# One layer of a hybrid mLSTM/HGRN2 block on one core: later use of the mixers' outputs, three blocks of merge gates computed first, small work moved to ScalarE

## The chip, the cores and the metric

The kernel runs on one core of a Trainium2 chip. A core has TensorE (PE, matrix products into PSUM), VectorE (DVE), ScalarE (ACT) and GpSimd (POOL), which run apart from each other and meet through semaphores, and a queue (SP) that issues transfers from memory. The metric is the device time of one execution in microseconds. Before the change it is 2555.0 us, the median of three runs (2554.29 to 2555.2).

## What is computed

The reference is one decoder layer in fp32 on 256 positions of width 2048:

```
x = x + 0.5 * swiglu(rmsnorm(x), ffn1)                       # inner width 5632
h = rmsnorm(x)
mq,mk,mv,mo,mi,mf,hq,hf,hi,hg,gate_m,gate_h = split(h @ w_in) # 2048 x 11272
y_m = mlstm_mixer(mq,mk,mv,mo,mi,mf)       # causal conv on q,k; 4 heads; 1024 wide
y_h = hgrn2_mixer(hq,hf,hi,hg)             # f = lb+(1-lb)*sigmoid(hf); 8 heads; 1024 wide
merged = sigmoid(gate_m)*(y_m @ w_proj_m) + sigmoid(gate_h)*(y_h @ w_proj_h)
x = x + merged @ w_out
x = x + cross_attention(rmsnorm(x), rmsnorm(mem))            # 4 heads of 512, 256 memory rows
x = x + 0.5 * swiglu(rmsnorm(x), ffn2)
out = rmsnorm(x)
```

Both mixers are written as scans over chunks. mLSTM weights a score q·k by an exponential of running sums of log forget gates, and divides by a guarded row sum. HGRN2 does the same with one decay for each of its 128 channels.

## The kernel before, in words

**Products.** Every large product has the 256 positions as rows (two blocks of 128, so two PSUM tiles `pa`) and 512 columns of the weight at a time. Each fp32 operand is split into a high and a low part, and three products stand for one: high·high, high·low, low·high (lines 248, 249, 250). Weights come by SP in tiles `wr` of four k-tiles (1 MB); each half of such a tile, two k-tiles, is one **group**: ACT casts it to the high part `wh`, DVE subtracts to get the low part `wl`, and PE then runs 2 k-tiles x 2 row blocks x 3 products = 12 matmuls on it. `wh` and `wl` have four buffers each, and a group is split three ahead of its use. There are 904 groups, counted here from 0: 264 for the first FFN, 264 to 511 for the mixer, 512 to 639 for cross attention, 640 to 903 for the second FFN. In the mixer: f and q of HGRN2 264 to 295, its v and g to 327, the mLSTM output gate in three narrower blocks of 344 columns 328 to 351, mLSTM q, k, v 352 to 383, then four merge blocks of 24 groups each from 384 (8 for `gm`, 8 for `gh`, 4 for y_h @ w_proj_h, 4 for y_m @ w_proj_m), and w_out from 480.

**The other operand** is needed transposed, as a pair `oh`, `ol`. `turn_on_vector` makes it from a 128x512x2 tile with 16 DVE transposes of 32x256 into `tt` (four pieces of four), then an ACT pass for `oh` and a DVE pass for `ol`. `written` holds the recording back until a pair that a matmul asks for has its instructions recorded.

**Order of the work around the products.** The kernel is recorded by a planner in Python. After each group `tick` adds the group's estimated PE time and lets small pieces in: pieces with a due time (`timed`), and a queue (`bg`) of mixer pieces, up to three for each group. Both only go in while the estimated backlog of DVE and ACT is under 2 us. The estimate is kept by `Paced`: a base and a time per element for each instruction of DVE and of ACT. What a piece records on PE, DVE and ACT then lies between the weight splits. A scheduler then assigns buffers and may still shift single instructions. All engines run in their recorded order.

**The pieces that matter here.** `hgrn_levels` (the decays, products `qc` with `kt`), `hgrn_out` (`hsq`, `hss`, `rstd` on POOL, then `g`, and the turn of y_h in two pairs), `mlstm_weights` (for each head: `di` = identity x input gate, `r0` and `r1` from it, four matmuls, then `ew`; `di`, `r0`, `r1` have one buffer each), `conv` (`mq`, `mk`), `mlstm_scores`, `mlstm_out` (the heads' `mo`, and the turn of y_m in two pairs). Right after the gates of merge block 0 a step calls `flush`: all pieces that are left are recorded there at once. Long-lived tiles (norm operands, y pairs, gates, `tt`) share one pool `s4` of 22 buffers.

Of the kernel before, what the change touches and what calls it, by code (L numbers as in the profile page):

```python
# [14 lines left out]
AF = mybir.ActivationFunctionType  # L15
ALU = mybir.AluOpType
# [3 lines left out]
P = 128  # L20
# [79 lines left out]
class Core:  # L100
    def __init__(self, nc):
        self.tensor, self.gpsimd, self.sync = nc.tensor, nc.gpsimd, nc.sync
        self.vector, self.scalar = Paced(nc.vector, 0.13, 0.00106), Paced(nc.scalar, 0.22, 0.00082)


class Block:
# [71 lines left out]
    def next_timed(self):  # L178
        i = min(range(len(self.timed)), key=lambda i: self.timed[i][0])
        self.timed.pop(i)[1]()  # L180

    def flush(self):
        while self.timed or self.bg:
            if self.timed:
                self.next_timed()
            else:
                self.bg.popleft()()

    def load(self, u, parts=1):
        if u.raw is None:  # L190
# [32 lines left out]
        self.flush()  # L223

    def gemm_nat(self, ops, wap, n0, n, evac, kts=None, row0=0, late=0):

        nc = self.nc
        box = {}  # L230
        pairs = ops
        nkt = 4 * len(pairs) if kts is None else kts

        def mm_for(k0, nk):
            def mm(hi, lo, ts=(0, 1)):
                if k0 == 0:
                    box["ps"] = [self.pacc([P, n]) for _ in range(2)]
                if k0 >= nkt - 2 * late and len(ts) == 2:
                    ts = (0,)
                    box.setdefault("late", []).append(lambda: mm(hi, lo, (1,)))  # L240
                for j in range(nk):
                    kt = k0 + j
                    xh, xl = self.written(pairs[kt // 4])
                    for t in ts:
                        sl = slice(t * P, (t + 1) * P)
                        a_h, a_l = xh[:, kt % 4, sl], xl[:, kt % 4, sl]
                        o = box["ps"][t]
                        nc.tensor.matmul(o, a_h, hi[:, j, :], start=(kt == 0), stop=False)  # L248
                        nc.tensor.matmul(o, a_h, lo[:, j, :], start=False, stop=False)  # L249
                        nc.tensor.matmul(o, a_l, hi[:, j, :], start=False, stop=(kt == nkt - 1))  # L250
            return mm

        for k0 in range(0, nkt, 4):
            u = Unit(wap, row0 + k0 * P, 4, n0, n, 2)
            for q in range(2):
                self.steps.append(Sub(u, q, mm_for(k0 + 2 * q, 2)))
        if not late:
            self.do(lambda: evac(box["ps"]))
            return

        def finish():
            evac(box["ps"], (0,))
            for f in box["late"]:
                f()
            evac(box["ps"], (1,))
        self.do(finish)
# [27 lines left out]
        self.unwritten[id(p)] = p  # L294
        return p

    def written(self, p):

        while id(p) in self.unwritten:
            self.next_timed()  # L300
        return p

    def turn_later(self, src, gain, dst, ticks=1):
        self.after(ticks, lambda: self.turn(src, gain, dst, (0,)))
# [137 lines left out]
    def rstd_of(self, ss, n, dim):  # L442
        nc = self.nc
        ms = self.sm(n, "ms")
        nc.vector.tensor_scalar(ms, ss, 1.0 / dim, EPS, op0=ALU.mult, op1=ALU.add)
        r = self.sm(n, "rstd", tag=f"rstd{n}")
        nc.gpsimd.tensor_tensor(r, ms, self.mhalf[:, :n], op=ALU.pow)  # L447
        return r

    def squares(self, src, ss_col):  # L450
# [79 lines left out]
    def mixer(self, norm, chunk_done):  # L530
        nc, a = self.nc, self.a
        w = a["w_in"][0]
        ops = LazyOps(lambda: norm().ops)
# [77 lines left out]
        self.do(lambda: self.bg.extend(self.mlstm_out(M, MV, MO)))  # L611


        merged = [None] * 4
        G = {}
        for c in range(4):
            for key, base in (("gm", 7176), ("gh", 9224)):
                def evac_g(ps, key=key):
                    r = norm().rstd
                    G[key] = self.t4([P, 2, 512], name=key)  # L620
                    for t in range(2):
                        nc.scalar.activation(G[key][:, t, :], ps[t], AF.Sigmoid, scale=r[:, t:t + 1])
                self.gemm_nat(ops, w, base + 512 * c, 512, evac_g)
            if c == 0:
                self.do(lambda: self.flush())

            def evac_h(ps):
                for t in range(2):
                    nc.vector.tensor_mul(G["gh"][:, t, :], ps[t], G["gh"][:, t, :])

            def evac_m(ps, c=c):
                gm, gh = G["gm"], G["gh"]
                for t in range(2):
                    nc.vector.tensor_mul(gm[:, t, :], ps[t], gm[:, t, :])
                    nc.vector.tensor_add(gm[:, t, :], gm[:, t, :], gh[:, t, :])
                merged[c] = self.pair()
                if c < 3:
                    self.turn_on_vector(gm, None, merged[c])
                else:
                    self.turn_later(lambda t: gm[:, t, :], None, merged[c])  # L640

            self.gemm_nat(LazyOps(lambda: self.Y["h"], 2), a["w_proj_h"][0], 512 * c, 512, evac_h)
            self.gemm_nat(LazyOps(lambda: self.Y["m"], 2), a["w_proj_m"][0], 512 * c, 512, evac_m)
        for c in range(4):
            def evac(ps, c=c):
                self.add_to_x(c, ps, 1.0, lambda: chunk_done(c))
            self.gemm_nat(LazyOps(lambda: merged, 4), a["w_out"][0], 512 * c, 512, evac)

    def hgrn_levels(self, h, b):


        nc = self.nc
# [9 lines left out]
        def prep_f():  # L662
            f = h["f"]
            for i in range(4):
                hd = 4 * b + i
                nc.vector.tensor_scalar(f[:, i, :], f[:, i, :], self.oml[:, hd:hd + 1], self.lb[:, hd:hd + 1],
                                        op0=ALU.mult, op1=ALU.add)

        def prep_k():
            S["k"] = self.t4([P, 4, T], name="k")  # L670
# [128 lines left out]
    def mlstm_weights(self, m):  # L799

        nc = self.nc
# [15 lines left out]
        def head(h):  # L817
            lf = [m["lf"][:, t, h:h + 1] for t in range(2)]
            ig = [gs[:, t, h:h + 1] for t in range(2)]
            di = self.small.tile([P, P], F32, name=self.nm("di"), tag="di", bufs=1)  # L820
            r0 = self.small.tile([P, 129], F32, name=self.nm("r0"), tag="r0", bufs=1)
            r1 = self.small.tile([P, 257], F32, name=self.nm("r1"), tag="r1", bufs=1)
            for t, r, o in ((0, r0, 0), (1, r1, 129)):
                nc.vector.tensor_scalar(di, self.ident, ig[t], None, op0=ALU.mult)
                nc.vector.scalar_tensor_tensor(r[:, o:o + P], in0=self.gt, scalar=lf[t], in1=di,
                                               op0=ALU.mult, op1=ALU.add)
            nc.vector.tensor_copy(r0[:, 128:129], lf[0])
            nc.vector.tensor_copy(r1[:, 0:129], lf[1].broadcast_to([P, 129]))
            p0 = self.ps([P, 129])
            p1 = self.ps([P, 257])  # L830
            nc.tensor.matmul(p0, self.le, r0, start=True, stop=True)
# [12 lines left out]
        return [logs] + [lambda h=h: head(h) for h in range(4)]  # L844

    def mlstm_scores(self, m):
# [330 lines left out]
```

## Time and profile before

| | before |
|---|---|
| median of 3 runs | 2555.0 us |
| profiled execution, its own time | 2555.04 us |
| its span, first to last instruction | 2553.2 us |
| PE busy | 2528.8 us, 99% |
| DVE busy | 1730.7 us, 68% |
| ACT busy | 1201.8 us, 47% |
| DMA, mean share of 16 engines | 57% |
| mean granted TensorE clock | 0.998 |

A busy PE is not PE at its peak: a matmul's shown duration (0.39 us) is longer than the distance to the next (0.227 us), so a stretch can be full and still slow. The number of matmuls in a stretch tells more than its busy time. A window's row has, after the stretch, its length, and for each engine the busy time with the number of instructions in brackets, then the granted clock, the DMA share and GB/s.

In this profile group 364 starts at 1016.8 us, group 405 at 1145.2 us, and the scores of the first attention head at 1575.4 us.

### The profile page before, as it was taken

What the parts mean: (1) busy time and instruction counts of PE and PEld (TensorE: products, weight loads), DVE (VectorE), ACT (ScalarE), POOL (GpSimd) and SP (SyncE); (2) the same over time, 40 slices, a digit from 0 to 9 for tenths busy, and PEclk for the clock granted to TensorE, in tenths of its full rate; (3) what the DMA queues carried; (4) which work ended last, traced back from release to release, by engine and by line L of the source; (5) the groups of instructions that cost most, each with busy time, mean ns of one, the idle gap of its engine ahead of it and who ended that gap; (6) DMA issues with size and microseconds to landing.
All of it is one profiled execution on the core that took longest, in us unless ns stands there. A gap on an engine that the chain in (4) does not pass through costs nothing.

```text
span 2553.2 us, 29044 instructions
## 1 busy us (share of the span) xinstructions
PE 2528.8 (99%) x11431; PEld 2104.7 (82%) x11431; DVE 1730.7 (68%) x2384; ACT 1201.8 (47%) x1385; POOL 13.5 (1%) x21
## 2 busy tenths in 40 slices
PE   8999999999999999999999999999999999999998
PEld 7888888888888898787888888888888888888887
DVE  5767644767768878967666787677767574457664
ACT  5444434444455565644444454444544443344443
POOL 0000000000000000000000000000000000000000
PEclk9999999999999999999999999999999999999999
DMA  7665565565555545545555565555566556555653
GB/s 262 197 193 189 195 198 190 189 198 190 193 190 185 176 138 165 183 163 181 190 191 197 187 212 180 170 175 173 190 198 190 191 196 197 188 192 194 214 189 128
DMA packets 243305, 479.92 MB, mean 188 GB/s; under 512 B 8008, under 2 KB 14432, under 8 KB 243168
## 3 DMA queue, kind: packets, MB, share of 16 engines
q1 hardware_dynamic: 242016, 476.15, 57.4%
q10 hardware_dynamic: 1152, 1.92, 0.2%
q8 instruction: 89, 1.46, 0.2%
q14 instruction: 48, 0.39, 0.0%
HBM read 475.94 MB, written 2.10 MB: 187 GB/s over the span
## 4 chain that ended last, share of the span: by engine, by line
PE 92%; DVE 6%; issue 1%; ACT 0%; DMA 0%; POOL 0%; SPq 0%; POOLq 0%; ACTq 0%
PE pa L250 30%; PE pa L248 30%; PE pa L249 30%; DVE wl L90 2%; DVE tt L90 2%; PE ps L726 1%; DVE ol L90 1%; DVE cv L90 0%; PE ps L277 0%; DMA x<-in_x 0%; PE ps L966 0%; PE ps L967 0%; PE ps L965 0%; POOL rstd L447 0%; ACT kn L90 0%
## 5 line engine op out<-in xcount | busy, mean ns | idle before, releaser
L90 DVE TENSOR_TENSOR wl<-wr,wh 128x1024 fp32r<-128x1024 f32 (+1 forms) x904 | 1094.2, 1213 | 721.6 <-ACT wh L90 715.0
L90 ACT CAST wh<-wr 128x1024 fp32r<-128x1024 f32 (+1 forms) x904 | 942.0, 1045 | 1141.9 <-PE pa L250 1091.3
L248 PE MATMUL pa<-wh,oh 128*128 128x512 f32 (+1 forms) x3616 | 1409.7, 390 | 7.0 <-ACT oh L90 4.4
L249 PE MATMUL pa<-wl,oh 128*128 128x512 f32 (+1 forms) x3616 | 1403.6, 388 | 2.3 <-DVE wl L90 2.3
L250 PE MATMUL pa<-wh,ol 128*128 128x512 f32 (+1 forms) x3616 | 1402.5, 388 | 0.2 <-DVE ol L90 0.2
L248 PEld LDWEIGHTS pa<-wh,oh 128*128 128x128 f32 x3616 | 680.0, 188 | 143.3 <-ACT oh L90 4.8
L249 PEld LDWEIGHTS pa<-wl,oh 128*128 128x128 f32 x3616 | 680.2, 188 | 141.1 <-DVE wl L90 5.5
L250 PEld LDWEIGHTS pa<-wh,ol 128*128 128x128 f32 x3616 | 679.7, 188 | 138.8 <-DVE ol L90 0.7
L90 DVE STREAM_TRANSPOSE tt<-sil 32x256 f32<-32x256 f32 x352 | 153.6, 436 | 6.8
L90 DVE STREAM_TRANSPOSE tt<-x 32x256 f32<-32x256 f32 x144 | 62.8, 436 | 2.8
L90 ACT CAST oh<-tt 128x1024 fp32r<-128x1024 f32 x29 | 30.6, 1054 | 39.7 <-DVE tt L90 39.7
L90 ACT ACT_TABLE_LOAD x34 | 43.6, 1283 | 10.1 <-DVE rs L90 3.1
L90 ACT ACTIVATE oh<-tt,cols 128x256 fp32r<-128x256 f32 x52 | 23.3, 500 | 47.7 <-DVE tt L90 47.7
L90 ACT ACTIVATE sil<-pa,rstd 128x512 f32<-128x512 f32 x44 | 29.8, 689 | 17.8 <-PE pa L250 17.7
L90 DVE TENSOR_TENSOR ol<-tt,oh 128x1024 fp32r<-128x1024 f32 x29 | 35.4, 1220 | 1.6 <-ACT oh L90 1.4
L90 DVE STREAM_TRANSPOSE tt<-kn 32x256 f32<-32x256 f32 x64 | 27.9, 436 | 5.6 <-ACT kn L90 4.5
L90 DVE SCALAR_TENSOR_TENSOR sil<-pa,rstd,sil 128x512 f32<-128x512 f32 x44 | 31.0, 743 | 0.0
L90 DVE STREAM_TRANSPOSE qt<-qn 32x256 f32<-32x256 f32 x64 | 27.9, 436 | 4.1 <-ACT qn L90 3.0
L90 ACT ACTIVATE oh<-ps,cols 128x256 fp32r<-128x256 f32 x44 | 20.3, 473 | 21.4 <-DVE ol L90 15.6
L90 DVE COPY_PREDICATED at<-cst,ps 128x128 f32<-128x128 int32 x80 | 22.8, 328 | 10.6 <-PE ps L726 10.0
L90 ACT ACTIVATE junk<-x 128x512 f32<-128x512 f32 x40 | 24.9, 625 | 7.6 <-DVE x L90 7.0
L90 DVE SCALAR_TENSOR_TENSOR ol<-ps,cols,oh 128x256 fp32r<-128x256 f32 x44 | 20.7, 480 | 10.8 <-ACT oh L90 10.5
(174 smaller groups left out, 649.4 us busy)
## 6 DMA issues: line engine op xcount, KB each, us to landing
wr<-in_ffn_w SPq DMA_DIRECT2D x263, 1024.0 KB, 5.2
wr<-in_w_in SPq DMA_DIRECT2D x80, 1024.0 KB, 5.1
wr<-in_xattn_wkv SPq DMA_DIRECT2D x32, 1024.0 KB, 5.4
wr<-in_w_out SPq DMA_DIRECT2D x16, 1024.0 KB, 5.1
wr<-in_xattn_wq SPq DMA_DIRECT2D x16, 1024.0 KB, 5.0
wr<-in_xattn_wo SPq DMA_DIRECT2D x16, 1024.0 KB, 5.1
wr<-in_w_in SPq DMA_DIRECT2D x12, 688.0 KB, 4.1
wr<-in_w_proj_h SPq DMA_DIRECT2D x8, 1024.0 KB, 5.0
```

The lines of the kernel that those rows point to most:

```text
L90: return fn(out, *args, **kw)
L248: nc.tensor.matmul(o, a_h, hi[:, j, :], start=(kt == 0), stop=False)
L249: nc.tensor.matmul(o, a_h, lo[:, j, :], start=False, stop=False)
L250: nc.tensor.matmul(o, a_l, hi[:, j, :], start=False, stop=(kt == nkt - 1))
L726: nc.tensor.matmul(ps[:, i, :], kt[:, g, j * P:(j + 1) * P], S["qc"][:, 2 * g + j, :], start=True, stop=True)
```

## The change

1. `flush` after the first merge gates is gone. `written` now takes the list and an index; while the pair isn't there, or not recorded yet, it records one more waiting piece (`next_piece`) and looks again.
2. The merge is split in `gates(c)` and `merge(c)`. The order becomes gates 0, 1, 2, merge 0, gates 3, merge 1, 2, 3. `gm` and `gh` are kept for each block, so up to six gate tiles live at once instead of two. y_h @ w_proj_h now starts at group 432 instead of 400.
3. `Paced` has new constants (DVE 0.19 + 0.00104 n instead of 0.13 + 0.00106 n; ACT 0.25 + 0.00085 n instead of 0.22 + 0.00082 n), and `rstd_of` adds 0.9 to DVE's estimate for the trip to POOL. Nothing that runs is changed by this directly, but the planner puts the pieces elsewhere.
4. 24 instructions go from DVE to ACT: `f` = lb + (1-lb)f (8 of 128x256), `di` (8 of 128x128), and the copies of `lf` into `r0` (4 of 128x1) and `r1` (4 of 128x129). ACT gets one ACT_TABLE_LOAD more, 35 instead of 34.

PE's number of instructions is the same.

```diff
-        self.vector, self.scalar = Paced(nc.vector, 0.13, 0.00106), Paced(nc.scalar, 0.22, 0.00082)
+        self.vector, self.scalar = Paced(nc.vector, 0.19, 0.00104), Paced(nc.scalar, 0.25, 0.00085)
...
+    def next_piece(self):
+        if self.timed:
+            self.next_timed()
+        else:
+            self.bg.popleft()()
...
-                    xh, xl = self.written(pairs[kt // 4])
+                    xh, xl = self.written(pairs, kt // 4)
...
-    def written(self, p):
-
-        while id(p) in self.unwritten:
-            self.next_timed()
-        return p
+    def written(self, ops, i):
+
+        while ops[i] is None or id(ops[i]) in self.unwritten:
+            self.next_piece()
+        return ops[i]
...
         nc.gpsimd.tensor_tensor(r, ms, self.mhalf[:, :n], op=ALU.pow)
+        nc.vector.end += 0.9
...
-        for c in range(4):
+        def gates(c):
             for key, base in (("gm", 7176), ("gh", 9224)):
                 def evac_g(ps, key=key):
                     r = norm().rstd
-                    G[key] = self.t4([P, 2, 512], name=key)
+                    g = G[key, c] = self.t4([P, 2, 512], name=key)
...
-            if c == 0:
-                self.do(lambda: self.flush())
...
+        for c in range(3):
+            gates(c)
+        merge(0)
+        gates(3)
+        for c in range(1, 4):
+            merge(c)
...
-                nc.vector.tensor_scalar(f[:, i, :], f[:, i, :], self.oml[:, hd:hd + 1], self.lb[:, hd:hd + 1],
-                                        op0=ALU.mult, op1=ALU.add)
+                nc.scalar.activation(f[:, i, :], f[:, i, :], AF.Identity, scale=self.oml[:, hd:hd + 1],
+                                     bias=self.lb[:, hd:hd + 1])
...
-                nc.vector.tensor_scalar(di, self.ident, ig[t], None, op0=ALU.mult)
+                nc.scalar.activation(di, self.ident, AF.Copy, scale=ig[t])
...
-            nc.vector.tensor_copy(r0[:, 128:129], lf[0])
-            nc.vector.tensor_copy(r1[:, 0:129], lf[1].broadcast_to([P, 129]))
+            nc.scalar.copy(r0[:, 128:129], lf[0])
+            nc.scalar.copy(r1[:, 0:129], lf[1].broadcast_to([P, 129]))
```

How the recorded order moves is shown at three places, on DVE. A `wl` row is the weight split of one group, so the rows between two `wl` are what the planner put in between. Digits behind a name are buffer numbers.

**The first place** is the end of HGRN2, from the split of group 361 in the kernel before: `hss`, `ms`, `g` are the head norm of one row block, `tt<-g` the transposes of y_h.

```order
L90 TENSOR_TENSOR wl_7383<-wr_7259,wh_7382 128x1024
L90 TENSOR_REDUCE hss_7372<-hsq_7370 128x4
L90 TENSOR_SCALAR ms_7374<-hss_7372 128x4
L90 SCALAR_TENSOR_TENSOR g_6673<-ps_7365,rstd_7376,g_6673 128x128 x4
L90 TENSOR_TENSOR wl_7422<-wr_7301,wh_7421 128x1024
L90 TENSOR_REDUCE hss_7409<-hsq_7407 128x4
L90 TENSOR_SCALAR ms_7411<-hss_7409 128x4
L90 SCALAR_TENSOR_TENSOR g_6673<-ps_7398,rstd_7413,g_6673 128x128 x4
L90 STREAM_TRANSPOSE tt_7487<-g_6673 32x2x4x32
```

Now, from the split of group 368:

```order
L90 TENSOR_TENSOR wl_7461<-wr_7377,wh_7460 128x1024
L90 TENSOR_TENSOR wl_7498<-wr_7377,wh_7497 128x1024
L90 TENSOR_REDUCE hss_7487<-hsq_7485 128x4
L90 TENSOR_SCALAR ms_7489<-hss_7487 128x4
L90 SCALAR_TENSOR_TENSOR g_6443<-ps_7476,rstd_7491,g_6443 128x128 x4
L90 TENSOR_TENSOR wl_7516<-wr_7419,wh_7515 128x1024
L90 STREAM_TRANSPOSE tt_7554<-g_6443 32x2x4x32 x4
L90 STREAM_TRANSPOSE cv_7559<-k_7533 32x2x4x32 x3
```

Before, both head norms of y_h's second pair stood in neighbouring groups (361 and 362), ahead of 32 transposes, 16 of that pair and 16 of the conv input (`cv<-q`). Now the piece there belongs to the first pair: its two head norms lie six groups apart (363 and 369), and 32 transposes (`tt<-g`, `cv<-k`) follow in groups 370 to 376. The second pair comes later, with head norms in groups 382 and 384 and its 16 transposes in groups 384 to 386.

**The second place** is the end of mLSTM, from the split of group 404 before: the last head's `mo`, the 16 transposes of y_m's second pair, its low part `ol`.

```order
L90 TENSOR_TENSOR wl_8551<-wr_8364,wh_8550 128x1024
L90 TENSOR_SCALAR ms_8495<-mss_8488 128x2
L90 TENSOR_TENSOR mrr_8499<-rstd_8497,den 128x2
L90 TENSOR_TENSOR wl_8567<-wr_8364,wh_8566 128x1024
L90 SCALAR_TENSOR_TENSOR mo_6840<-ps_8484,mrr_8499,mo_6840 128x256 x2
L90 STREAM_TRANSPOSE tt_8505<-mo_6840 32x2x4x32 x16
L90 TENSOR_TENSOR wl_8585<-wr_8443,wh_8584 128x1024
L90 TENSOR_TENSOR gh_8465<-pa_8534,gh_8465 128x512
L90 SCALAR_TENSOR_TENSOR ol_8504<-tt_8505,cols,oh_8503 128x256 x4
```

Now, inside the split of group 427:

```order
L90 SCALAR_TENSOR_TENSOR mo_6813<-ps_8904,mrr_8919,mo_6813 128x256 x2
L90 STREAM_TRANSPOSE tt_8980<-mo_6813 32x2x4x32 x2
L90 TENSOR_TENSOR wl_8947<-wr_8840,wh_8946 128x1024
L90 STREAM_TRANSPOSE tt_8980<-mo_6813 32x2x4x32 x5
L90 TENSOR_TENSOR wl_8965<-wr_8840,wh_8964 128x1024
L90 STREAM_TRANSPOSE tt_8980<-mo_6813 32x2x4x32 x5
L90 TENSOR_TENSOR wl_8988<-wr_8886,wh_8987 128x1024
L90 STREAM_TRANSPOSE tt_8980<-mo_6813 32x2x4x32 x4
L90 TENSOR_TENSOR wl_9008<-wr_8886,wh_9007 128x1024
L90 SCALAR_TENSOR_TENSOR ol_8963<-tt_8980,cols,oh_8962 128x256 x4
```

The 16 transposes stood in one piece after the split of group 405, and PE needs the pair in group 406. Now they lie spread over groups 427 to 430, `ol` follows the split of group 431, and PE needs the pair in group 438.

**The third place** is the last mLSTM head's weights, before from the split of group 379 (its products on PE stand at the start of group 378); `ew`, `mt` read the head before, `r_1290` and `r_1291` are `r0` and `r1` of the last head (the rows of `mt` alone are left out).

```order
L90 ISA ew_7867,mt<-ps_7861,cst 128x129
L90 ISA ew_7867,mt<-ps_7862,cst 128x257
L90 SCALAR_TENSOR_TENSOR r_1290_7892<-cst,lf,di_7891 128x128
L90 TENSOR_SCALAR nmt<-mt 128x2
L90 COPY r_1290_7892<-lf 128x1
L90 TENSOR_SCALAR di_7891<-cst,gs_7231 128x128
L90 COPY r_1291_7893<-lf 128x129
L90 SCALAR_TENSOR_TENSOR r_1291_7893<-cst,lf,di_7891 128x128
```

Now, in the splits of groups 394 and 395 (rows of `mt` alone and repeats of `mq` are left out):

```order
L90 ISA ew_8128,mt<-ps_8122,cst 128x129
L90 SCALAR_TENSOR_TENSOR r_1333_8156<-cst,lf,di_8155 128x128
L90 SCALAR_TENSOR_TENSOR mq_7457<-cv_7372,cols,mq_7457 128x254
L90 ISA ew_8128,mt<-ps_8123,cst 128x257
L90 TENSOR_SCALAR nmt<-mt 128x2
L90 TENSOR_SCALAR mq_7457<-cv_7372,cols 128x256
L90 TENSOR_TENSOR wl_8138<-wr_7994,wh_8137 128x1024
L90 SCALAR_TENSOR_TENSOR mq_7457<-cv_7372,cols,mq_7457 128x253
L90 SCALAR_TENSOR_TENSOR r_1334_8157<-cst,lf,di_8155 128x128
```

`di` and the copies have left DVE for ACT; in their place eight conv instructions (`mq`) and one weight split lie between the first `ew` of the head before and the last head's `r1`. On PE that head's four products now stand three quarters through group 393, 21 matmuls behind those of the head before (at the start of group 392); before it was 12.

More of the change, by code (lines that the diff above doesn't have):

```diff
@@ L180, in next_timed @@
         self.timed.pop(i)[1]()
+    def next_piece(self):
[3 more added lines that the diff above has]
+            self.bg.popleft()()
     def flush(self):
         while self.timed or self.bg:
-            if self.timed:
-                self.next_timed()
-            else:
-                self.bg.popleft()()
+            self.next_piece()
     def load(self, u, parts=1):
@@ L295, in pair @@
         return p
-    def written(self, p):
-        while id(p) in self.unwritten:
-            self.next_timed()
-        return p
+    def written(self, ops, i):
+        while ops[i] is None or id(ops[i]) in self.unwritten:
+            self.next_piece()
+        return ops[i]
     def turn_later(self, src, gain, dst, ticks=1):
@@ L611, in mixer @@
         self.do(lambda: self.bg.extend(self.mlstm_out(M, MV, MO)))
-        merged = [None] * 4
-        G = {}
-        for c in range(4):
+        merged, G = [None] * 4, {}
+        def gates(c):
             for key, base in (("gm", 7176), ("gh", 9224)):
@@ L619, in evac_g, with merge, evac_m @@
                     r = norm().rstd
-                    G[key] = self.t4([P, 2, 512], name=key)
+                    g = G[key, c] = self.t4([P, 2, 512], name=key)
                     for t in range(2):
-                        nc.scalar.activation(G[key][:, t, :], ps[t], AF.Sigmoid, scale=r[:, t:t + 1])
+                        nc.scalar.activation(g[:, t, :], ps[t], AF.Sigmoid, scale=r[:, t:t + 1])
                 self.gemm_nat(ops, w, base + 512 * c, 512, evac_g)
-            if c == 0:
-                self.do(lambda: self.flush())
+        def merge(c):
             def evac_h(ps):
                 for t in range(2):
-                    nc.vector.tensor_mul(G["gh"][:, t, :], ps[t], G["gh"][:, t, :])
-            def evac_m(ps, c=c):
-                gm, gh = G["gm"], G["gh"]
+                    nc.vector.tensor_mul(G["gh", c][:, t, :], ps[t], G["gh", c][:, t, :])
+            def evac_m(ps):
+                gm, gh = G["gm", c], G["gh", c]
                 for t in range(2):
```

## Prediction

> **What bounds the kernel now.** I read the page first, then PE's waits, then windows around them.
>
> ```profile
> span 2553.2 us, 29044 instructions
> PE 2528.8 (99%) x11431; PEld 2104.7 (82%) x11431; DVE 1730.7 (68%) x2384; ACT 1201.8 (47%) x1385; POOL 13.5 (1%) x21
> PE 92%; DVE 6%; issue 1%; ACT 0%; DMA 0%; POOL 0%; SPq 0%; POOLq 0%; ACTq 0%
> ```
>
> PE is the bound: the chain that ended last is 92% PE. The change takes no matmul away, so it can only win PE's lost time. PE's waits by cause are small:
>
> ```profile
> PE pa L248 <- ACT oh L90: 4.4, 1, 4.4
> PE pa L249 <- DVE wl L90: 2.3, 5, 0.5
> PE pa L250 <- DVE ol L90: 0.2, 1, 0.2
> ```
>
> They understate it, since a matmul is shown longer than its distance to the next. So I count matmuls in windows (after the stretch: its length, PE busy with its count, granted clock, DMA share, GB/s):
>
> ```profile
> 100.00:400.00 300.00, 300.00 (x1325) 1.00 0.60 193
> 1016.80:1037.10 20.30, 18.01 (x74) 1.00 0.43 141
> 1145.10:1161.70 16.60, 11.94 (x38) 0.79 0.39 133
> 1153.00:1159.00 6.00, 5.76 (x13) 0.50 0.14 22
> ```
>
> Undisturbed, a matmul takes 300/1325 = 0.2264 us, a group of 12 2.72 us. The second window holds groups 364 to 369, 72 matmuls (two more hang over the edges), worth 16.3 us: **4.0 us lost**. The third holds groups 405 to 407, 36 matmuls worth 8.15 us: **8.4 us lost**, part of it because after the 4.4 us wait the granted clock is 0.50 for 6 us.
>
> The causes, on DVE:
>
> ```profile
> L90 DVE TENSOR_TENSOR wl<-wr,wh 128x1024 fp32r<-128x1024 f32 x9 | 11.0, 1222 | 0.2
> L90 DVE STREAM_TRANSPOSE tt<-g 32x256 f32<-32x256 f32 x16 | 7.0, 436 | 0.3
> L90 DVE STREAM_TRANSPOSE cv<-q 32x256 f32<-32x256 f32 x16 | 7.0, 436 | 0.3
> L90 DVE SCALAR_TENSOR_TENSOR g<-ps,rstd,g 128x128 f32<-128x128 f32 x8 | 2.3, 344 | 2.2 <-POOL rstd L447 2.2
> L90 DVE TENSOR_REDUCE hss<-hsq 128x4 f32<-128x512 f32 x1 | 0.7, 678 | 0.0
> L90 DVE TENSOR_SCALAR ms<-hss 128x4 f32<-128x4 f32 x1 | 0.2, 170 | 0.0
> ...
> DVE g L90 <- POOL rstd L447: 4.5, 4, 1.1
> ...
> 1144.71 7.18 DVE L90 STREAM_TRANSPOSE tt<-mo 32x256 f32<-32x256 f32 x16
> 1151.91 1.23 DVE L90 TENSOR_TENSOR wl<-wr,wh 128x1024 fp32r<-128x1024 f32 x1
> 1153.06 0.68 DVE L90 TENSOR_TENSOR gh<-pa,gh 128x512 f32<-128x512 f32 x1
> 1153.66 1.66 DVE L90 SCALAR_TENSOR_TENSOR ol<-tt,cols,oh 128x256 fp32r<-128x256 f32 x4
> ```
>
> In the first stretch (groups of DVE from 1005 to 1037 us) DVE is full and the split `wl` comes too late. In the second (order of time) 16 transposes recorded by the flush stand in front of a split and of the operand that PE needs now.
>
> **The change, part by part.**
>
> *The flush hole.* By the order, the last transposes of y_m now lie over groups 427 to 430, `ol` behind the split of group 431, and PE wants the pair in group 438: 7 groups, 19 us, where it took 7.18 + 1.23 + 1.66 us of DVE. The pieces there cost, with the split, 1.2 + 5 x 0.44 = 3.4 us a group at most against 2.72, for four groups, so DVE falls back by under 3 us. The hole goes, and the half clock with it: **-8.4**. What is late next would be the merge: merges 1 to 3 stand side by side now, and a merge puts six 128x512 passes, 16 transposes and one `ol` as large as a split on DVE, 6 x 0.68 + 16 x 0.44 + 1.2 = 12.3 us, beside eight splits, 9.8 us, in 8 x 2.72 = 21.8 us. That is even, with the pieces spread: 0.
>
> *The overfull stretch.* A split may run ahead as far as four buffers let it, so DVE can be late by three groups less one cast and one split: 8.15 - 1.05 - 1.22 = 5.9 us. The cast's row:
>
> ```profile
> L90 ACT CAST wh<-wr 128x1024 fp32r<-128x1024 f32 x73 | 75.9, 1048 | 76.5 <-PE pa L250 65.8 <-issue 7.0 <-DVE gm L90 2.1
> ```
>
> Before, groups 361 to 369 asked of DVE 9 x 1.22, 32 x 0.436, two head norms at about 0.68 + 0.17 + 1.1 (POOL's trip) + 4 x 0.344 = 3.3 each, and 1.4 of head weights: 33 us in 24.5. 8.5 over 5.9 is about 3 us late; 4.0 was lost. Now groups 369 to 376 ask for 8 x 1.22 + 32 x 0.436 + 3.3 = 27.0 in 21.8: 5.3 behind, within 5.9. Groups 384 to 386 with the second pair ask for 3 x 1.22 + 16 x 0.436 + 3.3 + 1.2 = 15.1 in 8.2, 7 behind, but five groups nearly without pieces and two of PE's own product groups precede, and these durations overlap by some 0.08 us each when back to back. So **-4.0**, and **+0.5** for what reappears (bounds 0 and 2).
>
> *Moved to ACT.* 8 x 0.414 + 8 x 0.282 + 8 x 0.186 = 7.1 us leave DVE. On ACT the nearest rows are 0.50 us for 128x256 and 0.41 for 128x129, so up to 11 us arrive:
>
> ```profile
> L90 DVE TENSOR_SCALAR f<-f,oml,lb x8: 408/414/422, 771.9 to 828.1; 128x256 f32<-128x256 f32 x8
> L90 DVE TENSOR_SCALAR di<-cst,gs x8: 277/282/289, 980.9 to 1061.1; 128x128 f32<-128x128 f32 x8
> L90 DVE COPY r<-lf x8: 146/186/224, 1000.8 to 1061.3; 128x1 f32<-128x1 f32 x4, 128x129 f32<-128x129 f32 x4
> L90 ACT ACTIVATE mq<-mq,cols 128x256 f32<-128x256 f32 x4 | 2.0, 508 | 0.0
> L90 ACT ACTIVATE ew<-ew,nmt 128x129 f32<-128x129 f32 x4 | 1.6, 406 | 8.0 <-DVE nmt L90 8.0
> L90 ACT ACT_TABLE_LOAD x11 | 14.1, 1283 | 0.2
> ```
>
> ACT has cover: from 960 to 1200 us (the `wh` row above) it waits 65.8 us for PE to free a weight buffer. Only at groups 393 to 397 is it tight: by the order it has five casts, four table loads, six exponentials, four `di` and copies, two gate passes, near 20 us in 14.5; a cast's lead of three groups less itself is 7.1, so nothing reaches PE: 0. Bounds 0 and +2. [...] This trace shows 14.1 us for 11 loads and 0.2 us idle around them, so the sum goes by the row.
>
> *The last head's weights.* On PE this head's products now stand 21 matmuls behind those of the head before, and `di`, `r0`, `r1` have one buffer each, so `r0` can't be written before those have run. From that head's `ew` to `r1` the order puts on DVE two `ew` and `mt`, `r0`, six `mq` of 0.48, two of 0.35, `nmt`, a split and `r1`: 0.70 + 0.16 + 0.35 + 2.86 + 0.69 + 0.16 + 1.22 + 0.35 = 6.5 us.
>
> ```profile
> L90 DVE SCALAR_TENSOR_TENSOR mq<-cv,cols,mq 128x255 f32<-128x255 f32 (+2 forms) x7 | 3.3, 477 | 0.0
> L90 DVE CUSTOM_DVE_ANT_0 ew<-ps,cst 128x129 f32<-128x129 f32 (+1 forms) x2 | 0.7, 352 | 0.0
> 1050.96 0.38 PE L831 MATMUL ps<-r,cst 128*128 128x129 f32 x2
> 1051.77 0.48 PE L248 MATMUL pa<-wh,oh 128*128 128x512 f32 x1
> 1060.71 0.39 PE L250 MATMUL pa<-wh,ol 128*128 128x512 f32 x1
> 1061.21 0.49 PE L831 MATMUL ps<-r,cst 128*128 128x129 f32 x2
> ```
>
> PE gives 0.8 (the head's products, 1050.96 to 1051.77) + 21 x 0.2264 = 5.6 us, and `r1` is wanted 0.45 later, while `ew` can start 0.5 in: 7.0 against 6.0. Overlap on DVE would close that; a DVE that is 1.5 us behind would add to it. I take **+1.0**, bounds 0 and 2.5. The wait that stood here before, 1061.21 - 1060.71 - 0.23 = 0.27, goes, with a smaller one at group 377: **-0.4**. Behind the waiting product stand all later groups of PE; DVE and ACT meanwhile catch up. Whether the wait also halves the clock the rows leave open: 0.5 us waits left it at 1.00, one of 4.4 did not. [...] By the rows it could cost 3 us more (6 us at 0.50, the last window above); I count none, since one 2.5 us wait is nearer to the short ones.
>
> *Attention, moved by the planner's numbers.* Each head's scores paid for a late `ol`:
>
> ```profile
> 1575.40 0.28 PE L965 MATMUL ps<-oh,oh 128*128 128x256 f32 x1
> 1575.81 0.38 PE L966 MATMUL ps<-ol,oh 128*128 128x256 f32 x1
> 1578.87 0.69 DVE L90 TENSOR_REDUCE mx<-ps 128x2 f32<-128x512 f32 x1 [0.84 <-PE ps L967]
> 1582.56 0.62 DVE L90 TENSOR_SCALAR pr<-pr,sum 128x256 f32<-128x256 f32 x2
> ```
>
> 0.41 instead of 0.12 us, and 0.1 behind it: 0.39, four heads, 1.6. They now stand one group later (559 for 558) while `ol` keeps its place, so this goes. But the softmax `pr` takes 1582.56 + 0.62 - 1578.87 = 4.3 us, and its transposes now follow 19 matmuls later (4.3 us) instead of 24: 0 to 0.4 each, I take 0.15. Together **-1.0**.
>
> **Sum:** -8.4 - 4.0 - 0.4 - 1.0 + 0.5 + 1.0 = -12.3, against the profiled execution's 2555.04 us (1.8 above its span, 0.04 above the median): **2542.7 us**. With every new cost at nothing it is 2540.6, with all at their upper ends (2, 2, 2.5, 1.6 us) 2547.2; that is the forecast's own range.
>
> **The rivals.**
>
> *The lateness only moves (20%).* DVE's pieces are the same but for 7 us, and two of the new heaps (369 to 376, 384 to 386) use up the reserve in my sums. If each ran over by 2 us and the last head waited 2.5 with a slow clock behind it, 6 to 8 us come back: 2547 to 2550. For it: the reserve is thin. Against it: the same sums made the old stretch 3 late, and it was 4.
>
> *The change doesn't reach the hole (10%).* If y_m's second pair were still late at group 438, the hole would only move with the merge; then 4 us or less are won elsewhere and lost to the new waits: 2551 to 2556. Against it stand the 7 groups.
>
> *A round trip per head (7%), slower.* `di` is made by ACT and read by DVE, then overwritten by ACT for the next row block, with casts and table loads between. If each of the four heads' products, at groups 383, 390, 392 and 393, waited 3 us or more for `r0` or `r1` and the clock halved behind it (3 us), 4 x 6 = 24 us would outweigh the 13.8 won: near 2565. It decides from a wait of some 4 us a head. Against it: only the last head has under three groups between its products and its `r1` in the order.
>
> **How the numbers follow.** Chances: forecast 63%, moved lateness 20%, not reached 10%, round trip 7%. Two measurements of this kernel can be told apart from about 0.2%, 5.1 us. The forecast and most of the first rival are faster by more, 82%; the second and the rest of the first within, 12%; the third slower, 6%. The range is 2539.8 to 2550.5: below, the sum without new costs and 0.8 for what my windows miss; above, the first rival's end.
>
> **What would show it.** In the changed profile: no wait of PE for ACT `oh` over 1 us after 1000 us; a clock of 1.00 in every slice between 100 and 2500 us; no row "PE pa <- DVE wl" of 2 us; a wait "PE ps <- DVE r" of 0 to 2.5 us near group 393; in attention, waits for `ol` gone and short ones for `pr`. The forecast is wrong if PE still loses over 5 us between groups 360 and 440, or if merges 1 to 3 (456 to 479) lose anything.

## The result

The changed kernel takes **2541.04 us** (median; 2540.59 to 2542.01), the kernel before 2554.64 us beside it: a ratio of 0.9948, 95% interval 0.9935 to 0.996, or 13.6 us less. The prediction was 2542.7 us in a range of 2539.8 to 2550.5, and faster by more than 0.2%.

The page of the changed kernel: the span, the engines, and the chain that ended last.

```profile
span 2539.3 us, 29048 instructions
PE 2522.1 (99%) x11431; PEld 2103.0 (83%) x11431; DVE 1726.5 (68%) x2360; ACT 1209.8 (48%) x1410; POOL 14.4 (1%) x21
PE 99%; DMA 0%; issue 0%; SPq 0%; DVE 0%; ACT 0%; ACTq 0%; POOLq 0%; POOL 0%
```

The chain was 92% PE and 6% DVE; now it is 99% PE, and DVE's share in it is 0%. PE's waits by cause, all there are (in us: total, how many, the longest):

```profile
PE ps L383 <- DMA stage<-in_norm_ffn: 5.2, 1, 5.2
PE pa L250 <- ACT wh L90: 2.7, 1, 2.7
PE ps L279 <- DMA x<-in_x: 0.4, 1, 0.4
```

All three lie at the kernel's start. The rows for ACT `oh`, DVE `wl` and DVE `ol` are gone, and none for `r` has come.

Where the time came from is seen by cutting both traces at the same groups. The first stretch goes from the start of group 260 to that of group 484 (the end of the heads, the gates and the merges), the second from there to group 640 (attention and what follows). After each stretch stand its length, PE busy with its count, then the other engines, the granted clock, the DMA share and GB/s. Before:

```profile
723.79:1369.43 645.64, 638.59 (x2981) 538.18 (x2980) 483.78 (x805) 337.30 (x401) 9.38 (x11) 0.99 0.54 177
1369.43:1825.23 455.80, 455.26 (x2121) 379.89 (x2120) 342.33 (x495) 228.38 (x305) 1.40 (x2) 1.00 0.58 184
```

After:

```profile
723.25:1356.06 632.81, 632.81 (x2982) 537.14 (x2980) 479.57 (x781) 345.74 (x426) 9.37 (x11) 1.00 0.55 181
1356.06:1811.26 455.20, 455.20 (x2122) 379.65 (x2120) 342.49 (x496) 227.98 (x305) 2.31 (x2) 1.00 0.58 184
```

The same matmuls take 645.64 - 632.81 = **12.8 us** less in the first stretch and 455.80 - 455.20 = **0.6 us** less in the second. That is 13.4 us; the remaining 0.5 us of the two profiles lies ahead of group 260, which starts at 723.25 us instead of 723.79. In the new first stretch PE is busy all of its 632.81 us at a clock of 1.00, so no wait is left there. What remains are changes between small and large matmuls: behind the last head's products, for example, the first large matmul is followed after 0.31 us (1100.01 to 1100.32) instead of 0.23.

### The profile page after: what moved, and what is told of

Read it like the earlier page. It is cut to its first block, busy times and chain, and to the rows that moved or that the text cites. A ratio compares the mean times of both kernels' runs of the same rounds, so it can differ in the third digit from the quotient of the medians.

```text
span 2539.3 us, 29048 instructions
## 1 busy us (share of the span) xinstructions
PE 2522.1 (99%) x11431; PEld 2103.0 (83%) x11431; DVE 1726.5 (68%) x2360; ACT 1209.8 (48%) x1410; POOL 14.4 (1%) x21
## 4 chain that ended last, share of the span: by engine, by line
PE 99%; DMA 0%; issue 0%; SPq 0%; DVE 0%; ACT 0%; ACTq 0%; POOLq 0%; POOL 0%
PE pa L251 32%; PE pa L252 32%; PE pa L250 32%; PE ps L735 1%; PE ps L279 0%; DMA x<-in_x 0%; PE ps L975 0%; PE ps L976 0%; PE ps L974 0%; PE ps L1049 0%; PE ps L780 0%; PE ps L779 0%; PE ps L777 0%; PE ps L756 0%; PE ps L865 0%
```

## The experiments

The change has three parts, and I tried each of them alone, and the whole without the ACT moves: the **order** (three blocks of gates ahead of the first merge, operands forced out on demand, no flush), the planner's **numbers** (its costs of DVE and ACT and the 0.9 us after POOL's step), and the **ACT moves** (`f`, `di` and the two `lf` copies).

### The order alone

The changed kernel with the old numbers and with `f`, `di` and the copies back on DVE:

```diff
-        self.vector, self.scalar = Paced(nc.vector, 0.19, 0.00104), Paced(nc.scalar, 0.25, 0.00085)
+        self.vector, self.scalar = Paced(nc.vector, 0.13, 0.00106), Paced(nc.scalar, 0.22, 0.00082)
...
-        nc.vector.end += 0.9
...
```

> The kernel before with only the order of the blocks changed (gates 0 to 2, merge 0, gates 3, merges 1 to 3, no flush, operands recorded on demand); planner numbers and the 24 small instructions as before. My theory: the flush hole (8.4 us) goes by this part alone, the overfull stretch at groups 364 to 369 (4.0 us) and attention's late ol (1.6 us) stay: ratio 0.9967, about 2546.2 us, with PE's waits for DVE wl still near 2.3 us. Rival (the planner's numbers are what counts): within 2 us of before. Rival (all of it comes from the order): 2541.

Measured: 2546.65 us, ratio 0.9967 (0.9956 to 0.9979). The wait by cause that is left in the mixer, and the two stretches:

```profile
PE pa L251 <- DVE wl L90: 2.3, 5, 0.5
```

```profile
724.18:1361.41 637.23, 634.77 (x2982) 536.53 (x2981) 483.69 (x805) 337.31 (x401) 9.37 (x11) 1.00 0.55 180
1361.41:1817.22 455.81, 455.26 (x2121) 380.01 (x2120) 342.40 (x495) 228.38 (x305) 1.39 (x2) 1.00 0.58 184
```

The first stretch is 645.64 - 637.23 = 8.4 us shorter than before: the flush hole, to the tenth. The five waits for `wl` of the overfull stretch stand as they did (2.3 us in total), and attention takes 455.81 us as before. So the order pays for the hole and for nothing else; the other 4.4 us of the first stretch and the 0.6 of attention come with the rest of the change.

### The numbers alone

The kernel before with only the new numbers:

```diff
-        self.vector, self.scalar = Paced(nc.vector, 0.13, 0.00106), Paced(nc.scalar, 0.22, 0.00082)
+        self.vector, self.scalar = Paced(nc.vector, 0.19, 0.00104), Paced(nc.scalar, 0.25, 0.00085)
...
+        nc.vector.end += 0.9
```

> The kernel before with only the planner's new numbers (DVE 0.19 + 0.00104 n, ACT 0.25 + 0.00085 n, 0.9 for the POOL trip); flush after gates 0 kept. My theory: the overfull stretch (4.0) and attention's late ol (1.0 net) go, but the pieces that the new numbers put off pile up in the flush: by the order all four mLSTM heads' outputs now stand at group 403, with 32 transposes (14 us of DVE) and four head norms behind them, so the hole grows from 8.4 to some 20 us: 2562 us, 2557 to 2570. Rival (numbers alone are a gain, the pieces find room): 2549 to 2551.

Measured: 2561.91 us, ratio 1.0028 (1.0017 to 1.0039), **slower**. PE's wait by cause, the old place of the overfull stretch, and the hole with what follows it:

```profile
PE pa L248 <- ACT oh L90: 16.0, 2, 9.2
```

```profile
1015.00:1037.00 22.00, 22.00 (x107) 18.49 (x106) 18.23 (x36) 9.31 (x11) 2.01 (x2) 1.00 0.49 161
1136.00:1146.00 10.00, 1.21 (x6) 0.66 (x4) 8.89 (x25) 1.86 (x6) 0.69 (x1) 0.71 0.00 0
1154.00:1161.00 7.00, 0.49 (x3) 0.07 (x1) 6.78 (x16) 1.30 (x2) 0.00 (x0) 0.73 0.00 1
```

The numbers do empty the overfull stretch: PE is busy for all of its 22 us. But they do it by booking the work of the heads later, and with the old order the flush then has more to force out: PE waits 9.2 and 6.8 us for `oh` where it waited 4.4. The gain and the loss are the same work, moved. In the new order, with three blocks of gates between the heads and the first merge, there is room for it; the kernels with one and two blocks, below, show that fewer don't do.

### The ACT moves, taken out of the changed kernel

The changed kernel with the 24 instructions on DVE again, while the planner books them on ACT, so that the order stays:

```diff
-                nc.scalar.activation(f[:, i, :], f[:, i, :], AF.Identity, scale=self.oml[:, hd:hd + 1],
-                                     bias=self.lb[:, hd:hd + 1])
+                nc.scalar.end += 0.25 + 0.00085 * T
+                nc.vector.engine.tensor_scalar(f[:, i, :], f[:, i, :], self.oml[:, hd:hd + 1], self.lb[:, hd:hd + 1],
+                                               op0=ALU.mult, op1=ALU.add)
...
```

The same is done for `di` and the copies.

> The changed kernel with the 24 small instructions back on DVE while the planner still books them on ACT, so that the recorded order stays nearly the same. My theory: DVE has room in the new order, so 7 us more on it cost 0 to 1 us: 2541 to 2542, no PE wait for DVE wl. Rival (the 7 us taken off DVE are what emptied the overfull stretch): 3 to 4 us come back, 2544 to 2545, with waits for wl between groups 360 and 400.

Measured: 2541.11 us, ratio 0.9947 (0.9932 to 0.9962), the time of the changed kernel. Its page:

```profile
PE 2522.6 (99%) x11431; PEld 2103.5 (83%) x11431; DVE 1731.3 (68%) x2384; ACT 1202.5 (47%) x1386; POOL 14.4 (1%) x21
PE 99%; DMA 0%; issue 0%; SPq 0%; DVE 0%; ACT 0%; ACTq 0%; POOLq 0%; POOL 0%
```

DVE has its 5 us back (1731.3 for 1726.5) and the chain doesn't show it. In this order, where the work runs is worth nothing. (The order is the same but for the last head's products, which stand at group 393 instead of 393.75.) Whether the new costs alone would give this order, without the 24 instructions being booked on ACT, no run shows.

### The ACT moves alone, and two halves of them

The kernel before with the 24 instructions on ACT, old order and old numbers:

```diff
-                nc.vector.tensor_scalar(f[:, i, :], f[:, i, :], self.oml[:, hd:hd + 1], self.lb[:, hd:hd + 1],
-                                        op0=ALU.mult, op1=ALU.add)
+                nc.scalar.activation(f[:, i, :], f[:, i, :], AF.Identity, scale=self.oml[:, hd:hd + 1],
+                                     bias=self.lb[:, hd:hd + 1])
...
-                nc.vector.tensor_scalar(di, self.ident, ig[t], None, op0=ALU.mult)
+                nc.scalar.activation(di, self.ident, AF.Copy, scale=ig[t])
...
-            nc.vector.tensor_copy(r0[:, 128:129], lf[0])
+            nc.scalar.copy(r0[:, 128:129], lf[0])
...
```

> The kernel before with only the 24 small instructions on ACT. My theory: worth little by themselves; the planner moves pieces a bit, the overfull stretch loses at most its 2 us of head weights, and the flush hole stays at about 8 us: 2551 to 2556, ratio near 1. Rival (the moved work is the gain in the overfull stretch): 2550 to 2551 with no wait for DVE wl.

Measured: 2559.9 us, ratio 1.002 (1.0011 to 1.003). That is slower, beyond what was expected. The ten executions spread from 2556.47 us at a mean granted clock of 0.998 to 2560.98 at 0.996; the profiled one took 2558.05. PE's waits by cause, and the three longest for `r` (in square brackets PE's idle time and what ended it):

```profile
PE pa L249 <- DVE wl L90: 5.5, 5, 3.3
PE ps L834 <- DVE r L90: 2.7, 2, 1.7
PE ps L831 <- DVE r L90: 2.1, 1, 2.1
```

```profile
1046.24 0.49 PE L834 MATMUL ps<-r,cst 128*128 128x128 f32 x2 [1.68 <-DVE r L90]
1051.57 0.46 PE L831 MATMUL ps<-r,cst 128*128 128x129 f32 x2 [2.08 <-DVE r L90]
1053.69 0.49 PE L834 MATMUL ps<-r,cst 128*128 128x128 f32 x2 [1.03 <-DVE r L90]
```

The wait of 3.3 us for `wl` is the flush hole: groups 384 to 412 take 91.9 us here and 94.1 before. The loss lies ahead of it, in groups 340 to 384, which take 133.3 us for 126.9. There the heads' products wait for `r`. It looks like the prediction's third rival, the round trip per head, but the trace shows another cause. For the first of the three waits, ACT's `di` and DVE's `r` that reads it:

```profile
1034.53 0.40 ACT L90 ACTIVATE di<-cst,gs 128x128 f32<-128x128 f32 x1 [3.68 <-DVE r L90]
1045.83 0.35 DVE L90 SCALAR_TENSOR_TENSOR r<-cst,lf,di 128x128 f32<-128x128 f32 x1
```

`di` was done 10.9 us before DVE came to this `r`; for the other two it was 4.4 and 1.4 us. DVE wasn't waiting for ACT: it was busy all that time with what stands ahead of `r` in its recorded order, here above all 15 transposes of the conv and three weight splits. I split the edit to see whether `di` and the copies alone do it: the two halves of the diff above, each by itself on the kernel before.

> The kernel before with only the eight `f` passes on ACT (old order, old numbers). Theory (the loss of the kernel with all ACT moves alone, 2559.9, is the round trip of `di` and of the two `lf` copies between ACT and DVE): no loss, 2552 to 2556, no wait of PE for `r` over 0.6 us. Rival (ACT is too full or its order is upset, whichever pass is moved): 2557 to 2561.

> The kernel before with only `di` and the two `lf` copies on ACT, `f` left on DVE. Theory (round trip): 2557 to 2561, waits of PE for `r` of 1.5 us and more near 1045 to 1055 us. Rival (it is not the round trip): 2552 to 2556.

Measured: `f` alone 2556.8 us, ratio 1.0009 (1.0 to 1.0018, so its loss is at the edge of what these runs can tell); `di` and the copies alone 2557.57 us, ratio 1.0011 (1.0001 to 1.002). Neither theory held: the second time lies in the theory's range, though with waits half as long as it wanted, and the first lies between the two. Each half loses 2 to 3 us. Both have waits for `r`, and both keep the flush hole, as a wait of 5.3 us for `wl` (groups 384 to 412 take 94.3 and 94.5 us, 94.1 before). With `f` alone:

```profile
1048.29 0.49 PE L833 MATMUL ps<-r,cst 128*128 128x129 f32 x2 [0.48 <-DVE r L90]
1053.50 0.49 PE L833 MATMUL ps<-r,cst 128*128 128x129 f32 x2 [1.29 <-DVE r L90]
```

With `di` and the copies alone:

```profile
1057.43 0.49 PE L834 MATMUL ps<-r,cst 128*128 128x128 f32 x2 [0.36 <-DVE r L90]
1061.71 0.46 PE L831 MATMUL ps<-r,cst 128*128 128x129 f32 x2 [0.79 <-DVE r L90]
```

Since `f` alone leaves the whole making of `r` on DVE and still waits for it, ACT's part in the round trip isn't what all three share. What they share is how far back the heads' `r1` stands in DVE's order. With both on ACT, the `r1` of the second and third head stand behind the splits of groups 373 and 376, and PE wants them in groups 373 and 374; with `f` alone behind 374 and 377, for 374 and 375; with `di` and the copies the last two heads' behind 378 and 379, for 376 and 377. A group is split three ahead of its use at most, so an `r1` that stands two groups behind PE's place comes just in time or late, and the conv transposes ahead of it make DVE later still. One group behind cost little or nothing: before the change 378 for 377, and 379 for 378 with a wait of 0.1 us; in the changed kernel 393 for 392 and 395 for 393.75, with none. That this place in the order is the cause is my reading of these orders; no run moved the heads and nothing else. How close two heads' products stand on PE doesn't decide by itself: with the work put back on DVE the last two stand one group apart (392 and 393) without a wait, and the wait of 1.68 us above falls on a head five groups behind the one before it (373 and 368).

### Fewer blocks of gates ahead, and the flush put back

Three kernels change only the order of the blocks in the changed kernel. One block ahead, with the operands still forced out on demand:

```diff
-        for c in range(3):
-            gates(c)
-        merge(0)
-        gates(3)
-        for c in range(1, 4):
-            merge(c)
+        for c in range(4):
+            gates(c)
+            merge(c)
```

> The changed kernel with one block of gates ahead (gates 0, merge 0, gates 1, ...) and no flush: the mixer outputs are wanted at groups 400 to 406 as before the change, and the pieces recorded on demand. My theory: the new planner numbers put the pieces too late for that, so this is like the kernel before with the new numbers alone (2561.9): 2553 to 2563. Rival (recording on demand instead of the flush is the gain): 2541 to 2544.

Two blocks ahead:

```diff
-        for c in range(3):
-            gates(c)
-        merge(0)
-        gates(3)
-        for c in range(1, 4):
-            merge(c)
+        gates(0)
+        gates(1)
+        merge(0)
+        gates(2)
+        merge(1)
+        gates(3)
+        merge(2)
+        merge(3)
```

> The changed kernel with two blocks of gates ahead of merge 0 (then gates 2, merge 1, gates 3, merges 2, 3). By the order the last head stands at group 422 on PE and y_m's second pair is wanted there; with three blocks it is ready after the split of group 431. My theory: a hole of 5 to 10 us comes back: 2546 to 2552. Rival (two blocks are enough because the pieces are forced earlier without harm): 2541 to 2542.

The flush put back behind the first block of gates, three blocks ahead as in the change:

```diff
-        for c in range(3):
-            gates(c)
+        gates(0)
+        self.do(lambda: self.flush())
+        gates(1)
+        gates(2)
```

> The changed kernel with the flush put back behind gates 0, all else as changed (three blocks of gates still ahead). My theory: the flush records all four heads' outputs and the second pairs in one piece ahead of later weight splits, so DVE has some 25 us of pieces in front of them, against about 6 us of lead; PE loses 10 to 20 us and half-clock time: 2555 to 2565. Rival (what counts is only that the mixer outputs are wanted later): about 2541, since PE has other gates to compute.

Measured: one block 2559.1 us (ratio 1.0019, 1.0009 to 1.0028), two blocks 2553.49 us (0.9996, 0.9987 to 1.0006), the flush put back 2547.7 us (0.9972, 0.9962 to 0.9982). PE's wait by cause with one block, with two, and with the flush:

```profile
PE pa L250 <- ACT oh L90: 10.3, 2, 9.6
```

```profile
PE pa L250 <- ACT oh L90: 7.5, 2, 6.3
```

```profile
PE pa L251 <- DVE wl L90: 4.4, 1, 4.4
```

The hole shrinks with each block: 9.6 us, 6.3 us, none. Forcing out on demand doesn't close it by itself. With two blocks it is a little larger than I had allowed for, and the kernel gains nothing on the one before. The third kernel misses on both sides: neither 10 us and more, as I expected from the flush, nor nothing. Here PE has gates to work on behind the flush, so it doesn't wait for `oh`; it waits once for a split that stands behind the flushed pieces, 4.4 us, with a slow clock behind it:

```profile
1159.00:1163.00 4.00, 4.00 (x11) 3.14 (x12) 4.00 (x7) 3.46 (x6) 0.00 (x0) 0.57 0.06 7
```

That window loses 4.00 - 11 x 0.2264 = 1.5 us. Of the 6.6 us lost, 5.9 are this wait and this clock.

### Which wait slows the clock

The prediction left open whether a wait of 2.5 us halves the clock. In two kernels extra DVE passes over one weight split made PE wait in the early groups, where nothing else disturbs it. The first kernel's edit (the numbers are the split and how many passes; the second kernel has 26, 27, 28 and 30 passes at splits 25, 41, 57 and 73, and 23, 11 and 8 at 105 to 107):

```diff
         self.nc.vector.tensor_sub(s.lo, raw, s.hi.bitcast(F32))
+        self.count = getattr(self, "count", -1) + 1
+        for i in range({25: 17, 41: 19, 57: 21, 73: 23, 89: 25, 168: 22}.get(self.count, 0)):
+            half = s.lo[:, i % 2:i % 2 + 1, :]
+            self.nc.vector.engine.tensor_scalar(half, half.bitcast(F32), 1.0, None, op0=ALU.mult)
```

> The changed kernel with six forced waits of PE in the first FFN: after the weight split of groups 25, 41, 57, 73, 89 and 168, 17, 19, 21, 23, 25 and 22 more DVE passes over that split's result (128x512 each, value unchanged), so that PE should wait about 0.8, 1.6, 2.4, 3.2, 4.0 and 2.8 us at one place each, far apart. It asks from which length of a wait the granted clock drops. The rows before: waits up to 0.7 left it at 1.00, one of 4.4 dropped it to 0.50 for some 6 us. [...]

> The changed kernel with extra DVE passes that make PE wait at four places, far from each other, about 2.9, 3.2, 3.5 and 4.2 us, and at one place three times within 10 us, about 1.8, 2.2 and 1.2 us. The waits themselves make 2560. One theory: only the length of a single wait counts, with a bound between 2.5 us (which left the clock at 1.00) and 4.4 us (which halved it); then the clock stays at 1.00 behind the three short ones, and the time is 2560 plus 3 for each long one that halves. Rival: waits that follow each other closely add up, as in the kernel with the ACT moves alone; then the clock is 0.50 behind the third short one too, 3 us more.

Measured: 2549.71 us for the first and 2566.7 us for the second (one execution each, so only the traces are used). The first gave waits of up to 2.4 us, and none slowed the clock. Its longest, and the clock behind it:

```profile
265.12 0.50 PE L255 MATMUL pa<-wl,oh 128*128 128x512 f32 x1 [2.36 <-DVE wl L214]
```

```profile
265.10:268.00 2.90, 2.88 (x13) 2.39 (x14) 2.90 (x3) 0.28 (x1) 0.00 (x0) 1.00 0.02 6
```

The second, its five long waits in order of time:

```profile
87.28 0.80 PE L255 MATMUL pa<-wl,oh 128*128 128x512 f32 x1 [2.36 <-DVE wl L214]
135.64 0.80 PE L255 MATMUL pa<-wl,oh 128*128 128x512 f32 x1 [3.03 <-DVE wl L214]
185.34 0.50 PE L255 MATMUL pa<-wl,oh 128*128 128x512 f32 x1 [3.02 <-DVE wl L214]
234.47 0.80 PE L255 MATMUL pa<-wl,oh 128*128 128x512 f32 x1 [3.69 <-DVE wl L214]
330.77 0.50 PE L255 MATMUL pa<-wl,oh 128*128 128x512 f32 x1 [2.92 <-DVE wl L214]
```

And the clock behind each:

```profile
87.28:90.44 3.16, 3.16 (x8) 2.49 (x9) 3.16 (x4) 0.00 (x0) 0.00 (x0) 0.50 0.03 5
135.64:141.55 5.91, 5.91 (x14) 4.65 (x15) 3.50 (x4) 1.04 (x1) 0.00 (x0) 0.50 0.43 125
185.34:189.32 3.98, 3.98 (x11) 3.17 (x12) 3.68 (x4) 0.00 (x0) 0.00 (x0) 0.60 0.14 17
234.47:237.27 2.80, 2.80 (x7) 2.22 (x8) 2.80 (x4) 0.00 (x0) 0.00 (x0) 0.50 0.00 0
330.77:334.00 3.23, 3.23 (x14) 2.65 (x15) 3.23 (x9) 0.60 (x1) 0.00 (x0) 1.00 0.24 94
```

A wait of 2.36 us left the clock alone in one place and halved it in another; one of 2.92 left it alone, those of 3.02 and more halved it. So there is no single length from which it happens, and my theory of one bound between 2.5 and 4.4 us falls. (The 2.5 is the first kernel's 2.36 us counted from start to start of the matmuls, less the usual 0.23.) The three short waits in a row, which the rival needed, didn't come about (they came as 0.7, 0.3 and the 2.92 us, with full work between), so that question isn't answered by this kernel. In the kernel with the ACT moves alone the clock did halve after waits of 1.68, 2.08 and 1.03 us within 10 us: from 1056.14 to 1057.85 us its large matmuls start 0.43 us apart, where 0.23 is usual. A halving costs 3.16 - 8 x 0.2264 = 1.3 us in the first of these windows, 1.2 to 2.7 us in all of them.

## Why the prediction was right

By its steps, against the profiled executions:

- **The flush hole, -8.4:** right, shown by the order alone (645.64 - 637.23). What was to be late next, the merges, loses nothing: the whole stretch is 632.81 us of PE in 632.81.
- **The overfull stretch, -4.0, and +0.5 for what reappears, and the old wait for `r`, -0.4:** together -3.9 predicted. With the last head's term the first stretch is 12.83 - 8.41 = 4.4 us shorter than by the order alone, so the first and third of these are confirmed as a sum, and nothing reappeared. The reserve was thin, as I had worked out: I had 5.3 of 5.9 us used up in groups 369 to 376, so 0.6 left. Measured, the split for group 376 ends 1.4 us ahead of it, the least among these groups (1042.73 + 1.23 = 1043.96 against 1045.35):

```profile
1042.73 1.23 DVE L90 TENSOR_TENSOR wl<-wr,wh 128x1024 fp32r<-128x1024 f32 x1
1045.35 0.39 PE L250 MATMUL pa<-wh,oh 128*128 128x512 f32 x1
```

- **The last head's weights, +1.0:** the term that was mis-sized; it measured 0. Here are the first `ew` of the head before and the last `r` on DVE, and the product on PE that reads this `r`:

```profile
1094.12 0.28 DVE L90 CUSTOM_DVE_ANT_0 ew<-ps,cst 128x129 f32<-128x129 f32 x1
1099.04 0.35 DVE L90 SCALAR_TENSOR_TENSOR r<-cst,lf,di 128x128 f32<-128x128 f32 x1
1099.86 0.39 PE L843 MATMUL ps<-r,cst 128*128 128x128 f32 x2
```

I had 6.5 us from `ew` to the end of `r1`; it took 1099.04 + 0.35 - 1094.12 = 5.3. The sum added the durations as shown, but DVE starts its next instruction before the last one is shown to end (a 0.48 us `mq` is followed after 0.39 or 0.40), over 16 instructions. The prediction named this overlap and then didn't count it. This part of `r1` is done 1099.86 - 1099.39 = 0.47 us before the product that reads it, the head's fourth (the prediction took the third, which reads the copies that ACT made), so the term was nothing by a small margin.

- **Attention, -1.0:** the mechanism was right, the size a little off: 455.80 - 455.20 = 0.6. The waits for `ol` in the scores are gone, and a short one for `pr` has come: 0.38 us between these two starts where 0.23 is usual, so the 0.15 that I had taken. A change between small and large matmuls behind it, which I had not counted, takes the rest: 0.31 us instead of 0.23, four times.

```profile
1620.44 0.39 PE L250 MATMUL pa<-wh,oh 128*128 128x512 f32 x1
1620.82 0.72 PE L1049 MATMUL ps<-cst,pr 128*128 128x128 f32 x4
```

- **The ACT moves, 0:** right for this order, shown by the kernel with the work put back on DVE. The casts reached PE in time: PE's only wait for `wh` is the one of 2.7 us at the kernel's start. The 35 table loads took ACT 1.28 us each, and 31 of them are followed by its next instruction after 0.01 or 0.02 us.

Together -13.4 in the two stretches where -12.3 was predicted; the difference is the +1.0 and +0.5 for new waits that didn't come, less the 0.4 of attention. The other half microsecond by which the profile is shorter lies at the kernel's start, where nothing was predicted. One sum of the prediction is wrong: its four upper ends (2, 2, 2.5 and 1.6 us) on 2540.6 make 2548.7, not 2547.2; the stated range doesn't depend on it.

Of the rivals, *lateness only moves* and *not reached* are excluded by a PE without waits. *The round trip per head* was given 7% and didn't happen. In the old order the same ACT moves do cost 5.5 us at waits for `r`, but there DVE comes late by its own order, and ACT's `di` was ready. The reason I gave against it, that only the last head has under three groups between its products and its `r1`, is about the place in the order and not about ACT, and that place is also what the runs in the old order point to.

What I didn't foresee is how little the parts say of the whole. Against the kernel before beside them they are worth, alone, -7.7 (order), +7.5 (numbers) and +5.5 us (ACT moves), in sum +5.3; together -13.6. The prediction was right because it read the recorded order of the whole change and not the diff part by part.

## What to carry to other kernels

Where a planner's cost numbers set the order, cost the order that comes out, not the edits: moving an instruction that is itself free, or a truer cost, can put a step too far back in an engine's order and lose more than it wins. Work taken out of an overfull stretch has to go somewhere, so look for the place that must have room for it first (here three blocks of gates), and make both changes at once. When a chain on one engine is summed against a deadline of fractions of a microsecond, use the distances between starts, not the shown durations (here 5.3 us against the 6.5 that I had added up).

## What the runs showed of the hardware

The granted clock halved after a PE wait of 2.36 us (at 87.28 us) and stayed at 1.00 after one of 2.92 us (at 330.77 us), both in the second kernel with forced waits; in the first it stayed at 1.00 after another of 2.36 us (at 265.12 us). It halved after the waits of 3.02, 3.03 and 3.69 us in the second kernel, and after the one of 4.42 us before the change, where it was 0.50 for 6.8 us, from 1152.64 to 1159.46 us. So between 2.36 and 2.92 us the length of a wait didn't decide by itself. What does decide there, these runs don't show. The prediction counted no slow clock behind a wait of 2.5 us; behind the one of 2.36 us at 87.28 us a slow clock cost 1.3 us.
